# A decoder layer in float32 on one core: gate and up from seven half-size products instead of eight

## The chip, the cores and the metric

The kernel runs on one core of a Trainium2 chip. The metric is the device time in microseconds of one execution. A profiled execution leaves a trace, from which all rows below come.

## What is computed

One layer on 2048 tokens of 1024 values. Nearly all of its work is matrix products; the change touches the last line alone:

```python
h = rms_norm(x, attn_norm); proj = h @ w_in        # queries, keys, values, gates
y_dn = gated_deltanet_branch(...); y_swa = sliding_window_branch(...)
merged = gates[0] * (y_dn @ w_branch_dn) + gates[1] * (y_swa @ w_branch_swa)
x = x + merged @ w_out
h2 = rms_norm(x, ffn_norm)
x = x + (silu(h2 @ w_gate) * (h2 @ w_up)) @ w_down # D_FF = 2816
```

## The kernel before, in words

**Blocks.** The tokens are worked in four blocks of 512. Per block: the mixer (`mixer`: DeltaNet projections and cores, gates, branches), the output projection (`tok_gemm(("wo",))`), the norm before gate/up (`norm2`), then, for the *next* block, the key, value and query projections (`window_start`: `skv`, `sq`) and its sliding-window attention, and last gate/up and down in five parts of 4, 4, 4, 4 and 6 units. A unit f (`ffn_up`) is 128 rows of gate and of up, each the sum over eight slices of 128 inputs.

**Three products for one.** Every float32 operand is split into a high part `hi` in the rounded format float32r and the rest `lo = x - hi`; a product is hi·hi + hi·lo + lo·hi (`mm3`, L185). So a unit has 2 x 8 x 3 = 48 matmuls with 512 columns (tokens) moving over 128 x 128 weights.

**Weights.** `weights` (L154 to 183) gives the split weights. In block 0 it loads a raw tile `wraw` (2 buffers of 1 MB units), ACT copies out hi (L168), DVE or POOL in turn subtracts (L171), and the split tile `whl` is written to device memory (`wk`). Later blocks load `whl` as it is, 512 KB for half a unit of 1024 values. There are five `whl` buffers.

**Order.** TensorE's order is written by a planner: `drive` interleaves a dense generator (projections, gate/up, down) with side chains (attention, DeltaNet cores, norms), by an estimate of when each step is ready; the weight path goes by `self.raw` and is not in that estimate. The queues of ACT, DVE, POOL and of the DMAs (SP; some on ACT) are set by a scheduler. Every queue is in order. Tiles named `u` share `NU` slots; matmuls write eight banks (`acc`, `aux`).

**The end of a unit** (L889 to 904): ACT takes tanh of the gate's bank, DVE makes gate·(tanh + 1), multiplies by up's bank, ACT and DVE split the result into the pair `a` that down reads.

Most instructions carry line 109, which is the wrapper that records them; rows are told apart by their tiles: `h` the split activations, `a` the split result, `L`, `qT`, `kt`, `pT` attention's, `mt` the merged branches, `x` the residual.

Of the kernel before, what the change touches and what calls it, by code (L numbers as in the profile page):

```python
# [15 lines left out]
P = 128  # L16
# [12 lines left out]
NU = 63  # L29
ND = 6  # L30
WR = 2
WB = 5
PSUB = 2
# [81 lines left out]
class Emitter:  # L115
    def __init__(self, ctx, tc, ins, out, nblocks):
# [13 lines left out]
        self.kept = {}  # L130
        self.pacc = pool("acc", 8, space=bass.MemoryType.PSUM)
# [21 lines left out]

    def weights(self, key, a):  # L154
        nc = self.raw
        n = a * 264 if key[0] == "skv" else 1024
        h = a // 2
        hl = []
        if key not in self.kept:
            src = self.w_skv[key[1]] if key[0] == "skv" else self.w_all[UNITS[key]]  # L160
            raw = self.wp.tile([P, 1056], F32, name="wraw", tag="wraw", bufs=WR)
            nc.sync.dma_start(out=raw[:, :n], in_=src)
            keep = []
            for j in range(2):
                t = self.wp.tile([P, 2, 528], F32R, name="whl", tag="whl", bufs=WB)
                r = raw[:, j * n // 2:(j + 1) * n // 2]
                hi, lo = t[:, 0, :n // 2], t[:, 1, :n // 2]
                nc.scalar.activation(hi, r, AF.Copy)  # L168
                self.nsub += 1
                eng = nc.vector if self.nsub > 6 and self.nsub % PSUB else nc.gpsimd  # L170
                eng.tensor_tensor(out=lo, in0=r, in1=hi, op=ALU.subtract)  # L171
                if self.nblocks > 1:
                    d = self.kp.tile([P, 2, n // 2], F32, name="wk", tag="wk%d_%d" % (len(self.kept), j))
                    nc.sync.dma_start(out=d, in_=t[:, :, :n // 2].bitcast(F32))
                    keep.append(d)
                hl.append([t[:, e, :n // 2].rearrange("p (a m) -> p a m", a=h) for e in range(2)])
            self.kept[key] = keep
        else:
            for j in range(2):
                t = self.wp.tile([P, 2, 528], F32R, name="whl", tag="whl", bufs=WB)  # L180
                nc.sync.dma_start(out=t[:, :, :n // 2].bitcast(F32), in_=self.kept[key][j])
                hl.append([t[:, e, :n // 2].rearrange("p (a m) -> p a m", a=h) for e in range(2)])
        return lambda k: (hl[k // h][0][:, k % h], hl[k // h][1][:, k % h])
# [914 lines left out]
```

## Time and profile before

| | |
|---|---|
| median of 3 runs | 3195.55 us (3194.09 to 3197.91) |
| the profiled execution | 3196.13 us, its span 3194.3 us |
| busy: TensorE, VectorE, ScalarE, GpSimd | 3095.3, 1403.2, 837.6, 415.8 us |
| DMA | 596 MB, mean 187 GB/s |
| granted clock of TensorE | 0.99 on average |

The span runs from the first to the last instruction; the time is 1.8 us more. PE is TensorE's matmuls, PEld its weight loads, DVE VectorE, ACT ScalarE, POOL GpSimd. A matmul's busy time is its whole passage and overlaps the next one's; the distance from start to start is its pace. The 264-column projection (`skv`) of block 1 fills 1272 to 1280 us. In block 1 (the second block) the output projection begins at 1225 us, the attention of block 2 lies in 1325 to 1418, and the rest of gate/up and down goes to 1702; block 0 has the same stages from 441, 550 and 643 us on, and splits its weights there.

### The profile page before, as it was taken

The numbers are of one execution on the slowest core, as the hardware profiler recorded it, in microseconds if no ns is written. First come the engines' busy times: TensorE is split into PE (matmuls) and PEld (weight loads), VectorE is DVE, ScalarE is ACT, GpSimd is POOL, SyncE is SP. The second block draws the span as 40 slices with busy tenths as digits, with TensorE's granted clock in tenths as the row PEclk, the third lists the DMA queues.
The fourth block names the chain that finished last, engine by engine and source line by source line (L and its number), as shares of the span: only waits on it lengthen the run. The fifth ranks groups of instructions, "written<-read, shape, count | busy, mean of one in ns | idle before, by whom it ended". The sixth has DMA issues, their size and how long they took to land. (4 is left out here: it accounts for less than half of the span.)

```text
span 3194.3 us, 39761 instructions
## 1 busy us (share of the span) xinstructions
PE 3095.3 (97%) x14854; PEld 2523.6 (79%) x14854; DVE 1403.2 (44%) x3626; ACT 837.6 (26%) x2112; POOL 415.8 (13%) x401
## 2 busy tenths in 40 slices
PE   7888989999999999999999999999999999999999
PEld 5776778778888887878887888877888888878887
DVE  5867656533336544542215565443221655422221
ACT  4454334422323322330002323232000233110000
POOL 2433211322212100010001110011000211000000
PEclk9999999999999999999999999999999999999999
DMA  6554475588874446445556445545566544645565
GB/s 240 185 178 152 154 251 209 198 284 285 283 254 145 132 142 215 153 152 191 184 192 200 131 143 179 177 154 170 190 189 205 169 131 133 198 159 193 192 189 183
DMA packets 291848, 595.99 MB, mean 187 GB/s; under 512 B 18975, under 2 KB 20168, under 8 KB 291656
## 3 DMA queue, kind: packets, MB, share of 16 engines
q1 hardware_dynamic: 277648, 569.20, 54.1%
q10 hardware_dynamic: 14008, 24.25, 2.2%
q8 instruction: 117, 1.92, 0.2%
q14 instruction: 75, 0.61, 0.1%
HBM read 459.08 MB, written 134.30 MB: 186 GB/s over the span
## 5 line engine op out<-in xcount | busy, mean ns | idle before, releaser
L109 PE MATMUL acc<-h,whl 128*128 128x512 f32 x7296 | 1760.1, 397 | 7.5 <-DVE whl L171 4.9
L109 PEld LDWEIGHTS acc<-h,whl 128*128 128x128 f32 x7296 | 1357.6, 189 | 313.9 <-DVE whl L171 5.8
L109 PE MATMUL acc<-whl,a 128*128 128x512 f32 x2112 | 493.7, 393 | 0.0
L109 PEld LDWEIGHTS acc<-whl,a 128*128 128x128 f32 x2112 | 395.5, 188 | 90.3
L109 DVE TENSOR_TENSOR x<-x,acc 128x512 f32<-128x512 f32 x192 | 131.4, 687 | 390.4 <-PE acc L109 388.6
L171 POOL TENSOR_TENSOR whl<-wraw,whl 128x512 fp32r<-128x512 f32 (+1 forms) x123 | 167.0, 1359 | 565.4 <-ACT whl L168 472.6
L168 ACT ACTIVATE whl<-wraw 128x512 fp32r<-128x512 f32 (+1 forms) x240 | 149.0, 630 | 290.3 <-PE acc L109 136.1
L109 DVE TENSOR_TENSOR th<-th,acc 128x512 f32<-128x512 f32 x88 | 60.4, 687 | 316.0 <-PE acc L109 315.8
L109 DVE SCALAR_TENSOR_TENSOR th<-th,acc 128x512 f32<-128x512 f32 x88 | 60.5, 687 | 304.9 <-ACT th L109 304.9
L109 PE MATMUL acc<-whl,mt 128*128 128x512 f32 x768 | 181.9, 398 | 8.1 <-DVE h L109 7.6
L109 ACT ACTIVATE th<-acc 128x512 f32<-128x512 f32 x88 | 52.7, 598 | 499.5 <-PE acc L109 499.3
L109 PEld LDWEIGHTS acc<-whl,mt 128*128 128x128 f32 x768 | 145.9, 191 | 43.2 <-DVE h L109 8.5
L109 DVE SCALAR_TENSOR_TENSOR cv<-xr,cst_sb,cv 128x512 f32<-128x512 f32 x144 | 134.6, 935 | 60.7 <-ACT cv L109 53.1
L109 ACT ACTIVATE a<-th 128x512 fp32r<-128x512 f32 x88 | 55.5, 631 | 346.8 <-DVE th L109 332.1
L171 DVE TENSOR_TENSOR whl<-wraw,whl 128x512 fp32r<-128x512 f32 x117 | 89.8, 768 | 121.4 <-ACT whl L168 120.9
L109 PE MATMUL acc<-whl,h 128*128 128x264 f32 (+1 forms) x768 | 139.8, 341 | 0.0
L109 PEld LDWEIGHTS acc<-whl,h 128*128 128x128 f32 x768 | 118.0, 188 | 16.7 <-issue 1.1
L109 POOL COPY ccar<-xr 128x3 f32<-128x3 f32 x48 | 9.0, 188 | 858.5 <-ACT xr L109 858.5
L109 PE MATMUL acc<-sp,whl 128*128 128x512 f32 x384 | 103.2, 409 | 0.0
L109 POOL TENSOR_TENSOR pT<-pT,cst_sb 128x512 f32<-128x512 f32 x62 | 82.7, 1362 | 137.2 <-ACT pT L109 121.1
L109 ACT ACTIVATE L<-L,ast 128x256 f32<-128x256 f32 (+1 forms) x192 | 83.4, 457 | 60.0 <-DVE ast L109 60.0
L109 PE MATMUL acc<-ydn,whl 128*128 128x512 f32 x384 | 92.6, 401 | 0.4
(183 smaller groups left out, 2817.5 us busy)
## 6 DMA issues: line engine op xcount, KB each, us to landing
whl<-wk SPq DMA_DIRECT2D x708, 512.0 KB, 3.9
wk<-whl SPq DMA_DIRECT2D x236, 512.0 KB, 3.5
wraw<-in_w_all SPq DMA_DIRECT2D x118, 512.0 KB, 5.0
x<-in_x ACTq DMA_DIRECT2D x56, 256.0 KB, 5.1
out<-x ACTq DMA_DIRECT2D x32, 256.0 KB, 3.8
whl<-wk SPq DMA_DIRECT2D x12, 528.0 KB, 5.1
wk<-whl SPq DMA_DIRECT2D x4, 528.0 KB, 2.7
x<-in_x SPq DMA_DIRECT2D x8, 256.0 KB, 6.5
```

The lines of the kernel that those rows point to most:

```text
L109: r = f(*args, **kw)
L168: nc.scalar.activation(hi, r, AF.Copy)
L171: eng.tensor_tensor(out=lo, in0=r, in1=hi, op=ALU.subtract)
```

## The change

For blocks 1 to 3, gate and up of a unit are seen as a 2 x 2 matrix of quarters (A11, A12: gate, first and second half of the inputs; A21, A22: up) times a 2 x 2 matrix of the activations (B11, B12: first half of the inputs, tokens 0 to 255 and 256 to 511; B21, B22: second half). Seven products of quarters, with sums S1 to S4 of the weights and T1 to T4 of the activations, and seven additions on DVE and POOL of what they give replace the eight; each product is 4 x 3 matmuls of 256 columns (`ffn_seven`, `product`). The first two units of the last block (`PLAIN`) keep the eight products.

- Block 0 keeps the eight products, and also forms S1 to S4 of each unit (`four`: DVE two, POOL two) and writes these to device memory instead of split tiles.
- In later blocks a unit loads seven raw quarters of 256 KB (A11, A12, A22 from the input, S1 to S4 from device memory) and splits each (`seven`).
- `norm_S` forms and splits T1 to T4 after the norm (28 tiles of `u`); in the last block it also keeps the plain split for the two plain units.
- To make room, the activations `h` of the next block are written to device memory after `window_start` and read back when the last part's units are done (`refill`); both on ACT's DMA queue, 16 transfers of 256 KB each way, at three block ends.
- Raw tiles are half as large with eight buffers (`WR`), and stores of split tiles are issued after the next loads (`store_kept`).

The diff, cut to what the text below speaks of:

```diff
-NU = 63
+NU = 60
-WR = 2
+WR = 8
 WB = 5
+PLAIN = 2
...
+    def load_raw(self, src, n=TB):
+        raw = self.wp.tile([P, 528], F32, name="wraw", tag="wraw", bufs=WR)
+        self.raw.sync.dma_start(out=raw[:, :n], in_=src)
+        return raw[:, :n]
...
+    def split_raw(self, r, n=TB):
+        t = self.wp.tile([P, 2, 528], F32R, name="whl", tag="whl", bufs=WB)
+        hi, lo = t[:, 0, :n], t[:, 1, :n]
+        self.raw.scalar.activation(hi, r, AF.Copy)
+        self.either().tensor_tensor(out=lo, in0=r, in1=hi, op=ALU.subtract)
+        return t
...
+    def store_kept(self):
+        for d, t in self.unstored:
+            self.raw.sync.dma_start(out=d, in_=t)
+        self.unstored = []
...
+        if key in self.kept:
+            self.store_kept()
+            ts = [self.load_kept(d, n) for d in self.kept[key]]
+            raws = [self.load_raw(src[:, j * n:(j + 1) * n], n) for j in range(2)]
+            self.store_kept()
+            ts = [self.split_raw(r, n) for r in raws]
+            if self.nblocks > 1:
+                self.kept[key] = [self.keep(t[:, :, :n].bitcast(F32), [2, n]) for t in ts]
...
+    def four(self, keys):
+        v, gp = self.raw.vector, self.raw.gpsimd
+        got = {n: self.load_raw(self.quad(keys, m, h))
+               for n, m, h in (("A11", 0, 0), ("A12", 0, 1), ("A21", 1, 0), ("A22", 1, 1))}
+        self.store_kept()
+        def group(m):
+            hl = [[t[:, e, :TB].rearrange("p (a m) -> p a m", a=4) for e in range(2)]
+                  for t in [self.split_raw(got["A%d%d" % (m + 1, h + 1)]) for h in range(2)]]
+            return lambda k: (hl[k // 4][0][:, k % 4], hl[k // 4][1][:, k % 4])
+        def sums():
+            kept = self.kept[keys] = {}
+            for n, x, y, op, eng in (("S1", "A21", "A22", ALU.add, v), ("S2", "S1", "A11", ALU.subtract, v),
+                                     ("S3", "A11", "A21", ALU.subtract, gp), ("S4", "A12", "S2", ALU.subtract, gp)):
+                got[n] = self.u([TB], name="ws")
+                eng.tensor_tensor(out=got[n], in0=got[x], in1=got[y], op=op)
+                kept[n] = self.keep(got[n], [TB])
+        return group, sums
...
+    def seven(self, keys):
+        own = {"A11": (0, 0), "A12": (0, 1), "A22": (1, 1)}
+        self.store_kept()
+        def of(name):
+            t = self.split_raw(self.load_raw(self.quad(keys, *own[name]) if name in own else self.kept[keys][name]))
+            return [t[:, e, :TB].rearrange("p (a m) -> p a m", a=4) for e in range(2)]
+        return of
...
+    def product(self, ps, w, H, operand, start=True):
+        mm = self.nc.tensor.matmul
+        for k in range(4):
+            hi, lo = H[k][operand]
+            for i, (l, r) in enumerate(((w[0], hi), (w[0], lo), (w[1], hi))):
+                mm(ps, l[:, k], r, start=start and k == 0 and i == 0, stop=k == 3 and i == 2, skip_group_check=not start)
+            yield 0
...
+            f1, f2 = fs.pop(k), fs.pop(k + 4)
+            (b11, b12), (b21, b22) = [(f[:, 0], f[:, 1]) for f in (f1, f2)]
+            ta, tb = [self.u([2, 256], name="hs") for _ in range(2)]
+            gp.tensor_tensor(out=ta[:, 0], in0=b12, in1=b11, op=ALU.subtract)
+            gp.tensor_tensor(out=ta[:, 1], in0=b22, in1=ta[:, 0], op=ALU.subtract)
+            v.tensor_tensor(out=tb[:, 0], in0=b22, in1=b12, op=ALU.subtract)
+            v.tensor_tensor(out=tb[:, 1], in0=b21, in1=ta[:, 1], op=ALU.subtract)
+            if hs is None:
+                one = self.u([2, 256], F32R, name="hb")
+                nc.scalar.activation(one[:, 0], b11, AF.Copy)
+                v.tensor_tensor(out=one[:, 1], in0=b11, in1=one[:, 0], op=ALU.subtract)
+                o = {"B11": (one[:, 0], one[:, 1])}
+                two = split(f2, v)
+            else:
+                o = {"B11": tuple(e[:, 0:256] for e in hl[k])}
+                two = [e.rearrange("p (a n) -> p a n", a=2) for e in hl[k + 4]]
+            for names, (hi, lo) in ((("B21", "B22"), two), (("T1", "T2"), split(ta, v)), (("T3", "T4"), split(tb, gp))):
+                for i, n in enumerate(names):
+                    o[n] = (hi[:, i], lo[:, i])
...
+        if b == 0:
+            yield from self.norm_T(xns, self.g2, hs)
+        else:
+            yield from self.norm_S(xns, self.g2, H, hs if b + 1 == self.nblocks else None)
...
+        keys = (("up", f, 0), ("up", f, 1))
+        if b == 0:
+            group, sums = self.four(keys)
+        elif b + 1 == self.nblocks and f < PLAIN:
+            group, sums = lambda m: self.raw_weights(keys[m]), lambda: None
+        else:
+            return self.ffn_seven(H, keys)
+        return self.ffn_eight(hs, group, sums)
...
+        yield lambda: len(H) == 4
+        w = self.seven(keys)
+        half = (slice(0, 256), slice(256, 512))
+        bank = lambda: self.acc()[:, 0:256]
+        Y = bank()
+        yield from self.product(Y, w("S2"), H, "T2")
+        c = self.u([2, 256], name="pc")
+        nc.scalar.activation(c[:, 1], Y, AF.Copy)
+        G = bank()
+        yield from self.product(G, w("A11"), H, "B11")
+        nc.scalar.activation(c[:, 0], G, AF.Copy)
+        U = self.u([2, 256], name="pu")
+        gp.tensor_tensor(out=U[:, 0], in0=c[:, 0], in1=c[:, 1], op=ALU.add)
+        Z = bank()
+        yield from self.product(Z, w("S1"), H, "T1")
+        yield from self.product(Y, w("S3"), H, "T3", start=False)
+        v.tensor_tensor(out=U[:, 1], in0=c[:, 0], in1=Y, op=ALU.add)
+        th = self.u([TB], name="th")
+        up = self.u([TB], name="up")
+        v.tensor_tensor(out=up[:, half[1]], in0=U[:, 1], in1=Z, op=ALU.add)
+        yield from self.product(G, w("A12"), H, "B21", start=False)
+        nc.scalar.activation(th[:, half[0]], G, AF.Tanh, scale=0.5)
+        v.scalar_tensor_tensor(out=th[:, half[0]], in0=th[:, half[0]], scalar=1.0, in1=G, op0=ALU.add, op1=ALU.mult)
+        yield from self.product(Y, w("A22"), H, "T4", start=False)
+        v.tensor_tensor(out=up[:, half[0]], in0=c[:, 0], in1=Y, op=ALU.add)
+        yield from self.product(Z, w("S4"), H, "B22", start=False)
+        v.tensor_tensor(out=U[:, 0], in0=U[:, 0], in1=Z, op=ALU.add)
+        nc.scalar.activation(th[:, half[1]], U[:, 0], AF.Tanh, scale=0.5)
+        v.scalar_tensor_tensor(out=th[:, half[1]], in0=th[:, half[1]], scalar=1.0, in1=U[:, 0], op0=ALU.add, op1=ALU.mult)
+        v.tensor_tensor(out=th, in0=th, in1=up, op=ALU.mult)
+        return self.ffn_act(th)
...
+        if b:
+            self.put = []
+            for k, h in enumerate(hs):
+                self.put.append([])
+                for e in range(2):
+                    d = self.kp.tile([P, TB], F32, name="hk", tag="hk%d_%d" % (k, e))
+                    nc = self.raw
+                    nc.scalar.dma_start(out=d, in_=h[e].bitcast(F32))
+                    self.put[-1].append(d)
+            hs.clear()
+    def refill(self, hs):
+        for d in self.put:
+            h = self.pair("h")
+            for e in range(2):
+                self.raw.scalar.dma_start(out=h[e].bitcast(F32), in_=d[e])
+            hs.append(h)
+            yield 1500
...
-        yield lambda: kv.scales
+        yield lambda: kv.scales and len(hs) == KT
...
+                if last and more:
+                    h2.clear()
+                    h4.clear()
+                    self.spawn(self.refill(hs))
```

**How it moves instructions.** First TensorE in block 1, after attention, one part of four units and down's parts around it (`hb`: the split sums of the activations). Before:

```order
L109 MATMUL acc<-h,whl 128x512 x27
L109 MATMUL aux<-pT,vt 64x512 x4
L109 MATMUL acc<-h,whl 128x512 x123
L109 MATMUL acc<-whl,a 128x512 x96
L109 MATMUL acc<-h,whl 128x512 x192
L109 MATMUL acc<-whl,a 128x512 x96
```

After:

```order
L110 MATMUL acc<-hb,whl 128x256 x69
L110 MATMUL acc<-whl,a 128x512 x9
L110 MATMUL aux<-pT,vt 64x512 x4
L110 MATMUL acc<-whl,a 128x512 x87
L110 MATMUL acc<-hb,whl 128x256 x336
L110 MATMUL acc<-whl,a 128x512 x96
L110 MATMUL acc<-hb,whl 128x256 x336
```

Four units are 336 matmuls of 256 columns instead of 192 of 512; down's are the same.

Second ACT in the same part of block 1 (whole queue; `th` tanh, `a` the split result, `pc` the copies of the banks Y and G, `pu` and `acc` what tanh reads). Before:

```order
L109 ACTIVATE a_13257<-th_13224 128x512 [waits DVE_49]
L109 ACTIVATE th_13290<-acc_13265 128x512 [waits PE_49]
L109 ACTIVATE a_13323<-th_13290 128x512 [waits DVE_49,Activation_49]
L109 ACTIVATE th_13356<-acc_13331 128x512 [waits PE_49,Activation_49]
L109 ACTIVATE a_13389<-th_13356 128x512 [waits DVE_49,Activation_49]
```

After, a little more than one unit (the tile of A22, the result of the unit before, the two copies, S4, then the next unit's quarters):

```order
L110 ACTIVATE th_15678<-pu_15640 128x256 [waits DVE_49]
L169 ACTIVATE whl_15844<-wraw_15842 128x512 [waits DMAHW3_49,PE_49,Pool_49]
L110 ACTIVATE a_15739<-th_15678 128x512 [waits DVE_49]
L110 ACTIVATE pc_15761<-acc_15743 128x256
L110 ACTIVATE pc_15761<-acc_15763 128x256 [waits PE_49]
L169 ACTIVATE whl_15862<-wraw_15860 128x512 [waits DMAHW4_49,Activation_49]
L169 ACTIVATE whl_15888<-wraw_15886 128x512 [waits DMAHW5_49,PE_49,Pool_49]
L169 ACTIVATE whl_15908<-wraw_15906 128x512 [waits DMAHW6_49,PE_49,Activation_49]
L110 ACTIVATE th_15820<-acc_15763 128x256 [waits PE_49]
L169 ACTIVATE whl_15929<-wraw_15927 128x512 [waits DMAHW7_49,Pool_49]
L169 ACTIVATE whl_15946<-wraw_15944 128x512 [waits DMAHW0_49,DVE_49,PE_49]
L169 ACTIVATE whl_15967<-wraw_15965 128x512 [waits DMAHW1_49,PE_49,Pool_49]
```

Seven splits a unit and four steps of 256 columns stand where two instructions stood; the split of S4 comes behind the copies here, and ahead of them in every other unit.

Third ACT at the end of block 0's gate/up and in its last down part, where weights are split for the first time. Before:

```order
L109 ACTIVATE a<-th 128x512
L168 ACTIVATE whl<-wraw 128x512
L109 ACTIVATE th<-acc 128x512
L168 ACTIVATE whl<-wraw 128x512 x3
L109 ACTIVATE a<-th 128x512
L168 ACTIVATE whl<-wraw 128x512 x4
```

After:

```order
L110 ACTIVATE a<-th 128x512
L169 ACTIVATE whl<-wraw 128x512
L110 ACTIVATE th<-acc 128x512
L169 ACTIVATE whl<-wraw 128x512 x3
L110 ACTIVATE a<-th 128x512
L1120 DMA h<-hk 128x512 x16
L169 ACTIVATE whl<-wraw 128x512 x4
L1205 DMA out<-x 128x512 x2
```

All 16 transfers that bring `h` back stand ahead of seven of the twelve splits of this down part.

## Rows read from the trace of the kernel before

**Rows 1.** Page, part 1: busy time, share and instructions of each engine.

```profile
PE 3095.3 (97%) x14854; PEld 2523.6 (79%) x14854; DVE 1403.2 (44%) x3626; ACT 837.6 (26%) x2112; POOL 415.8 (13%) x401
```

**Rows 2.** Waits of TensorE, whole span: us in total, times, longest.

```profile
PE acc L109 <- DVE whl L171: 4.9, 2, 3.1
PE acc L109 <- POOL whl L171: 1.3, 1, 1.3
```

**Rows 3.** Timeline of TensorE, block 1, gate/up: start us, us, engine, what, count.

```profile
1468.81 44.65 PE L109 MATMUL acc<-h,whl 128*128 128x512 f32 x192
1513.30 22.33 PE L109 MATMUL acc<-whl,a 128*128 128x512 f32 x96
```

**Rows 4.** Windows: us; busy of PE, PEld, DVE, ACT, POOL; clock; DMA share; GB/s.

```profile
1272.00:1280.00 8.00, 8.00 (x68) 8.00 (x67) 5.40 (x21) 0.45 (x2) 0.00 (x0) 1.00 0.79 249
```

**Rows 5.** Timeline of TensorE, block 0, attention's score matmuls and the next group.

```profile
621.42 2.23 PE L109 MATMUL aux<-kt,qT 128*128 128x256 f32 x16
623.49 0.40 PE L109 MATMUL acc<-h,whl 128*128 128x512 f32 x1
```

**Rows 6.** Weight loads in 1272 to 1280 us: count | busy, mean ns | idle.

```profile
L109 PEld LDWEIGHTS acc<-whl,h 128*128 128x128 f32 x67 | 8.2, 188 | 0.0
```

**Rows 7.** Groups by line and shape: count | busy, mean ns | idle before.

```profile
L168 ACT ACTIVATE whl<-wraw 128x512 fp32r<-128x512 f32 x236 | 146.7, 630 | 290.0 <-PE acc L109 136.1 <-DMA wraw<-in_w_all 84.4 <-issue 48.7
L171 DVE TENSOR_TENSOR whl<-wraw,whl 128x512 fp32r<-128x512 f32 x117 | 89.8, 768 | 121.4 <-ACT whl L168 120.9
L171 POOL TENSOR_TENSOR whl<-wraw,whl 128x512 fp32r<-128x512 f32 x119 | 162.0, 1362 | 552.7 <-ACT whl L168 460.0 <-DVE G L109 26.3 <-PE aux L109 21.2
L109 ACT ACTIVATE T<-aux 64x256 f32<-64x256 f32 x16 | 6.0, 374 | 6.7 <-PE aux L109 6.2
L109 DVE TENSOR_TENSOR L<-L 128x256 f32<-128x256 f32 x60 | 25.2, 421 | 29.9 <-ACT L L109 29.1
L109 DVE TENSOR_TENSOR th<-th,acc 128x512 f32<-128x512 f32 x88 | 60.4, 687 | 316.0 <-PE acc L109 315.8
L109 ACT ACTIVATE L<-L,ast 128x256 f32<-128x256 f32 x120 | 59.4, 497 | 47.5 <-DVE ast L109 47.5
L109 DVE SCALAR_TENSOR_TENSOR h<-aux,cst_sb,h 128x512 fp32r<-128x512 f32 x64 | 43.7, 744 | 3.7 <-ACT h L109 3.2
```

**Rows 8.** Windows by stage; columns as in rows 4.

```profile
441.00:487.00 46.00, 43.55 (x189) 34.97 (x188) 15.70 (x24) 14.46 (x29) 7.97 (x6) 1.00 0.82 285
550.00:643.00 93.00, 87.49 (x405) 66.00 (x404) 52.64 (x167) 47.74 (x138) 37.78 (x31) 0.98 0.53 183
643.00:894.00 251.00, 251.00 (x1085) 203.67 (x1085) 81.04 (x120) 75.67 (x125) 58.70 (x46) 1.00 0.83 285
1224.00:1271.00 47.00, 46.10 (x194) 37.40 (x195) 10.18 (x15) 8.17 (x21) 0.00 (x0) 0.96 0.61 201
1325.00:1418.00 93.00, 92.15 (x458) 71.69 (x456) 46.72 (x170) 37.66 (x118) 22.03 (x21) 1.00 0.45 144
1418.00:1669.00 251.00, 251.00 (x1087) 203.81 (x1086) 50.93 (x76) 20.72 (x35) 0.00 (x0) 1.00 0.59 188
```

**Rows 9.** Timeline of TensorE, block 3: transposes, then the first gate/up.

```profile
2817.66 6.15 PE L109 MATMUL aux<-cst_sb,xn 128*128 128x128 f32 x32 [4.64 <-DVE xn L109]
2823.57 44.69 PE L109 MATMUL acc<-h,whl 128*128 128x512 f32 x192
```

**Rows 10.** ACT's DMA issues of x, 1200 to 1260 us: count: duration ns min/median/max.

```profile
L356 ACTq DMA_DIRECT2D x<-in_x x10: 334/361/680, 1200.5 to 1226.1; - x10
```

**Rows 11.** Timeline, block 1, the end of a unit of gate/up: DVE, then ACT, then DVE.

```profile
1491.28 0.69 DVE L109 TENSOR_TENSOR th<-th,acc 128x512 f32<-128x512 f32 x1 [4.23 <-PE acc L109]
1492.00 0.64 ACT L109 ACTIVATE a<-th 128x512 fp32r<-128x512 f32 x1 [5.67 <-DVE th L109]
1492.67 0.69 DVE L109 SCALAR_TENSOR_TENSOR a<-th,a 128x512 fp32r<-128x512 f32 x1 [0.70 <-ACT a L109]
```

More of the change, by code (lines that the diff above doesn't have):

```diff
@@ new lines, in keep, with load_kept @@
+    def keep(self, t, shape):
+        d = self.kp.tile([P] + shape, F32, name="wk", tag="wk%d" % self.nkept)
+        self.nkept += 1
+        self.unstored.append((d, t))
+        return d
+    def store_kept(self):
+        for d, t in self.unstored:
+            self.raw.sync.dma_start(out=d, in_=t)
+        self.unstored = []
+    def load_kept(self, d, n=TB):
+        t = self.wp.tile([P, 2, 528], F32R, name="whl", tag="whl", bufs=WB)
+        self.raw.sync.dma_start(out=t[:, :, :n].bitcast(F32), in_=d)
+        return t
@@ L154, in weights @@
     def weights(self, key, a):
-        nc = self.raw
-        n = a * 264 if key[0] == "skv" else 1024
+        n = (a * 264 if key[0] == "skv" else 1024) // 2
         h = a // 2
+        src = self.w_skv[key[1]] if key[0] == "skv" else self.w_all[UNITS[key]]
         hl = []
[L159 to L177, printed above, removed]
-        else:
[L179 to L182, printed above, removed]
@@ new lines, in weights, with quad @@
+        for t in ts:
+            hl.append([t[:, e, :n].rearrange("p (a m) -> p a m", a=h) for e in range(2)])
+        return lambda k: (hl[k // h][0][:, k % h], hl[k // h][1][:, k % h])
+    def quad(self, keys, m, h):
+        return self.w_all[UNITS[keys[m]]][:, h * TB:(h + 1) * TB]
+    def four(self, keys):
[15 more added lines that the diff above has]
+        return group, sums
@@ L351, in norm_T, with norm_S, turned, split @@
             yield 0
+    def norm_S(self, xns, gain, H, hs):
+        nc, v, gp = self.nc, self.nc.vector, self.nc.gpsimd
+        fs, hl = {}, {}
+        def turned(kk):
+            ps = self.aux()
+            for t in range(NT):
+                nc.tensor.transpose(ps[:, t * P:(t + 1) * P], xns[t][kk // 4][:, (kk % 4) * P:(kk % 4 + 1) * P], self.ident)
+            f = fs[kk] = self.u([2, 256], name="hf")
+            ff, g = f.rearrange("p a n -> p (a n)"), gain[:, kk:kk + 1]
+            if hs is None:
+                nc.scalar.activation(ff, ps, AF.Copy, scale=g)
+                return
+            hl[kk] = h = self.pair("h")
+            nc.scalar.activation(h[0], ps, AF.Copy, scale=g)
+            v.scalar_tensor_tensor(out=h[1], in0=ps, scalar=g, in1=h[0], op0=ALU.mult, op1=ALU.subtract)
+            if kk % 2:
+                nc.scalar.activation(ff, ps, AF.Copy, scale=g)
+            else:
+                v.tensor_scalar(out=ff, in0=ps, scalar1=g, scalar2=None, op0=ALU.mult)
+        def split(src, eng):
+            hi, lo = [self.u([2, 256], F32R, name="hb") for _ in range(2)]
+            nc.scalar.activation(hi, src, AF.Copy)
+            eng.tensor_tensor(out=lo, in0=src, in1=hi, op=ALU.subtract)
+            return hi, lo
+        if hs is not None:
+            for kk in range(KT):
+                turned(kk)
+                hs.append(hl[kk])
+                yield 0
+        for k in range(4):
+            for kk in (k, k + 4) if hs is None else ():
+                turned(kk)
+                yield 0
+            f1, f2 = fs.pop(k), fs.pop(k + 4)
[5 more added lines that the diff above has]
+            v.tensor_tensor(out=tb[:, 1], in0=b21, in1=ta[:, 1], op=ALU.subtract)
+            if hs is None:
+                one = self.u([2, 256], F32R, name="hb")
[9 more added lines that the diff above has]
+                    o[n] = (hi[:, i], lo[:, i])
+            H.append(o)
+            yield 0
@@ L378, in norm2 @@
         yield
-        yield from self.norm_T(xns, self.g2, hs)
+        if b == 0:
+            yield from self.norm_T(xns, self.g2, hs)
+        else:
+            yield from self.norm_S(xns, self.g2, H, hs if b + 1 == self.nblocks else None)
         yield
@@ L896, in ffn_up @@
         v.scalar_tensor_tensor(out=th, in0=th, scalar=1.0, in1=pg, op0=ALU.add, op1=ALU.mult)
-        w = self.weights(("up", f, 1), 8)
+        w = group(1)
+        sums()
         pu = self.acc()
```

32 lines of the change are left out of this document (23 added, 9 removed).

## The prediction

> **What bounds the kernel now.** I read the busy totals first: TensorE is busy for 97% of the span, and the next engine, VectorE, for 44% [rows 1]. Then the waits of TensorE: the long ones lie at the start, in the first block, and before the last block's gate/up; in the first block 4.9 and 1.3 us are waits for a weight tile that is still being split [rows 2]. So the time is the number of TensorE's instructions times their pace, and the pace is read from a stretch without gaps. In the second block's gate/up, 192 matmuls of 512 columns start at 1468.81 and the next stage starts at 1513.30: 44.49 / 192 = 0.2317 us each [rows 3]. One unit f (128 rows of gate and of up) has 48 of them, 11.12 us. A matmul's busy time is no pace, as the ends overlap the next start. Last I read the stages, for what lies idle beside TensorE [rows 8].
>
> **TensorE's gain.** 64 units (22, 22 and 20 in blocks 1, 2, 3, counted from 0) go from 48 matmuls of 512 columns to 84 of 256. The columns fall by an eighth; what matters is the price of 256. Three rows bound it. The 264-column projection ran 66 starts in 8.00 us (two of the 68 counted had begun before): 0.1212 [rows 4]; carried eight columns down along the line from 512 to 264 columns it is 0.1176. The attention's 16 score matmuls of 256 columns took 2.07 us from their first start to the next group, 0.1294 with their three changes of bank [rows 5]. I take 0.120, nearest the 264-column row, because a product is also a gapless run of twelve into one bank. A unit then costs 84 x 0.120 = 10.08 us and saves 1.04 us; 64 units save **66.6 us** (79 at 0.1176, 16 at 0.1294).
>
> In that 264-column stretch weight loads last 188 ns each [rows 6] while a new matmul starts every 121 ns and TensorE shows no gap: loads lie under earlier matmuls. [...]
>
> **The splits of the weights.** A unit in blocks 1 to 3 now loads seven raw quarters and splits each: ACT 7 x 0.630 = 4.4 us, and 3.5 subtractions each on DVE (0.768, 2.7 us) and POOL (1.362, 4.8 us) [rows 7]. Two copies and two tanh of 256 columns at 0.374 and the activation's 0.63 bring ACT to 6.5 us of 10.1; six DVE steps of 256 columns (0.421), a multiply and a difference (0.69 each) bring DVE to 6.6. No engine is full. A product lasts 1.44 us; five buffers leave four products, 5.8 us, between a freed buffer and its next use, against 0.63 + 1.36. Loads fall from 2.1 to 1.8 MB a unit. In the gapless stage I cost the splits at nothing; the cover is those 5.8 us.
>
> The tight place is ACT's turn. Product 4 adds into bank Y, so it waits for the copy of Y, which stands behind the last unit's activation and, in every other unit, behind the split of S4, which waits for product 2. Product 2 ends 2.9 us into the unit; 0.17 until its result is out (0.285 less 0.120), split 0.63, copy 0.37: 4.1 us, against product 4's start at 4.3. The other branch (DVE 0.42, tanh 0.37, DVE 0.42 and 0.69, ACT 0.63, hops of 0.03 to 0.1 [rows 11]) ends at 3.0 and fits too. I put **+2 us** for places where it doesn't; bounds 0 and the second rival.
>
> **Attention beside gate/up** (blocks 1 and 2). There ACT and DVE work for the attention's chain too, whose steps TensorE takes in a fixed order. Block 0 shows what splits do to it: in 550 to 643 us, with four splits a unit, TensorE was busy 87.49 of 93 us; in the same stage of block 1, without splits, 92.15 [rows 8]. So four splits cost 4.65 us, and seven in a shorter unit at 1.9 times the rate some 9. But the new order also leaves more matmuls between the chain's steps (75 short ones, 9.0 us, where 30 of 0.23, 7.0 us, stood). I take 7 a block, **+14 us** (bounds 0 and 59, the third rival).
>
> **Forming the activation's sums.** In block 3, eight transposed groups now get a third copy: DVE 0.744 plus half of a pass over a bank (0.687), against 0.77 a group before (6.15 / 8) [rows 7, 9]: +2.6 us. The sums lie under the two plain units (22 us). In blocks 1 and 2 they lie beside the 81 query matmuls (18.8 us); four rounds of about 3.8 us on ACT fit, and waiting banks cost 1 us each. **+4.6 us** (2 to 12).
>
> **The activations of the next block go out and come back.** 16 transfers of 262 KB each way, 4.2 MB, at three block ends, all issued by ACT at 0.36 us each [rows 10]. On the way out they lie in the output projection. In block 0 that stage moved 285 GB/s at a share of 0.82, so about 347 is full; 91 more is 376, and 17.3 MB take 50 us instead of 46: +4. In blocks 1 and 2, 201 + 89 fits [rows 8], but the activations behind these issues on ACT come later: +1 each. On the way back, block 0 has all 16 standing in ACT's queue before the split of the sixth of twelve down tiles. Issue alone holds ACT for 5.8 us, and waiting for half of them to land another 6; they start about 3 us into the part (the last unit's end chain above), and the sixth tile's split must begin at 9.8 us (two pairs of tiles at 24 x 0.2317, three matmuls, less 0.63 and 1.36): 0 to 5 late, I take 3. In the other blocks nothing of the part stands behind them, and 188 + 127 GB/s fits. **+9 us** (0 to 30).
>
> **Block 0.** Raw loads in halves with eight buffers, and stores behind the next loads, should remove most of the 6.2 us of waits for weights: **-4** (-6.2 to +3). The four sums a unit (DVE 2 x 0.69, POOL 2 x 1.36) lie under 11.1 us on engines that are 32% and 23% busy there [rows 8], and attention's part costs **+1** (0 to 8).
>
> **Sum.** -66.6 + 2 + 14 + 4.6 + 9 - 4 + 1 = -40.0. The profiled execution took 3196.1 us (span 3194.3 and 1.8 around it), 0.6 above the median of the runs: **3156 us**.
>
> **Rivals.**
> 1. Weight loads set the pace. At 188 ns a piece a unit costs 84 x 0.188 = 15.8 us, 4.7 more than before: 3196 + 300 + 27 = 3523 us. For it: TensorE's load row is busy for 8.00 of 8.00 us in the 264-column stretch. Against it: the same stretch has no gap at 121 ns. Chance 0.02. [...]
> 2. **Slower: ACT's turn sets the period.** If a subtraction of 0.77 on DVE stands before the add that ends product 7 and another before the multiply, the copy of Y comes 1.5 us later, 1.2 past product 4's start, in every unit: 77 us, 3233 us. It decides from 0.6 us past the margin on, as 40 us / 64 is what a unit has to lose. For it: in-order queues and a margin of 0.2 us. Against it: in the order of DVE these subtractions stand where ACT has already waited, and the hops are short. Chance 0.12.
> 3. No change: each of the eight attention tiles waits for a whole run of eight exponentials (4.0 us) and eight additions (3.4): 59 us instead of 14, 3201 us. For it: block 0's 5.5 idle us. Against it: the wider gaps. Chance 0.14.
> 4. The transfers are not hidden: 4.2 MB at 347 GB/s is 12 us, six times 72 instead of 9: 3219 us. Against it: the mean rate of a block doesn't rise. Chance 0.05.
>
> **How the numbers follow.** My forecast's own course has 0.67 and lies between 3125 (0.1176, half of the losses) and 3182 (0.1244 a matmul). With the third rival's 3201 the range is **3125 to 3205**; outside stay the other rivals and part of the low end. About 6 us (0.2%) is what a measurement tells from no change: faster is below 3189, slower above 3202. Faster: 0.67, half of rival 3 and a part of 4: 0.77. Slower: rivals 1 and 2, and parts of 3 and 4: 0.17. The same: 0.06.
>
> **What would show it.** In the second block's gapless gate/up: 336 matmuls of 256 columns in 40.3 us, four units, where 192 took 44.5. At 42 us or more the price or rival 2 is at work; then TensorE's waits name ACT or DVE behind `pc`, or a late weight tile. The stage from the query projection to the end of attention tells rival 3 by its idle time, block 0's last down part the refill, by a wait for a tile that ACT splits late. Fewer than 1 us saved a unit, or more than 20 us of new waits in attention, makes me wrong. [...]

## The result, and the profile after

The changed kernel took **3212.82 us** (median of 4 runs, 3209.78 to 3218.35) against 3195.79 in the same comparison: a ratio of 1.0059, 95% interval 1.0047 to 1.0071. It is slower by 17 us where I forecast 40 less. The profiled execution has a span of 3210.7 us, 16.4 more than before. Its busy totals, as [rows 1]:

```profile
PE 3054.8 (95%) x17158; PEld 2594.7 (81%) x17158; DVE 1831.4 (57%) x4258; ACT 1174.2 (37%) x2804; POOL 876.8 (27%) x773
```

TensorE is busy for 40 us less and the time is longer all the same: the gain was made, and idle time was put in. The table shows where: lengths of stages in us, from the starts of TensorE's matmuls in each trace (blocks 1 and 2 as a pair). The "attention stretch" runs from a block's first gate/up matmul to the first of the third down part: 12 units, two down parts, and in blocks 0 to 2 the next block's attention (the expectations below, which name its end loosely, mean this stretch). The "dense stretch" goes on to the last down part: 10 units, two down parts.

| stage | before | changed | a5: splits on DVE | a3: six split tiles | k2: best |
|---|---|---|---|---|---|
| block 0, up to gate/up | 515.4 | 514.4 | 490.8 | 512.2 | 485.1 |
| block 0, attention stretch | 210.5 | 216.6 | 210.3 | 213.6 | 220.5 |
| block 0, last down part | 33.0 | 41.4 | 42.0 | 41.2 | 33.6 |
| 1, 2: wo's end to gate/up | 40.5, 40.5 | 43.2, 43.2 | 41.7, 43.3 | 43.3, 41.7 | 43.3, 41.7 |
| 1, 2: attention stretch | 202.2, 202.3 | 213.6, 212.9 | 199.7, 199.4 | 205.5, 205.6 | 199.5, 198.2 |
| 1, 2: dense stretch | 155.4, 155.4 | 144.6, 145.9 | 144.4, 145.2 | 144.6, 146.1 | 143.0, 143.1 |
| 1, 2: last down part | 33.0, 33.0 | 36.2, 37.3 | 38.5, 39.3 | 33.1, 33.1 | 33.1, 33.1 |
| block 3, first stretch | 177.7 | 173.3 | 172.8 | 173.9 | 170.7 |
| block 3, dense stretch | 155.4 | 145.9 | 144.9 | 146.5 | 143.4 |
| block 3, last down part | 33.0 | 33.1 | 33.4 | 33.1 | 33.1 |

The dense stretches give what was forecast. In TensorE's timeline of block 1, four units (336 matmuls) go from 1501.24 to 1541.20, 0.1189 us a start, where [rows 3] had 44.49 us; two rows above stand the 5.15 us that were lost beside attention:

```profile
1334.32 0.96 PE L110 MATMUL acc<-hb,whl 128*128 128x256 f32 x6
1340.43 10.80 PE L110 MATMUL acc<-hb,whl 128*128 128x256 f32 x75 [5.15 <-DVE pu L110]
...
1501.24 40.12 PE L110 MATMUL acc<-hb,whl 128*128 128x256 f32 x336
1541.20 4.08 PE L110 MATMUL acc<-whl,a 128*128 128x512 f32 x17
```

The windows of block 1, columns as in [rows 4], say the same: 17.7 us without TensorE in the attention stretch (214 less 196.27), where the kernel before had 0.85, and almost none in the dense one. First the changed kernel, then the one before:

```profile
1327.00:1350.00 23.00, 17.85 (x134) 17.51 (x133) 17.54 (x33) 10.69 (x23) 7.64 (x7) 0.85 0.35 105
1327.00:1541.00 214.00, 196.27 (x1367) 176.32 (x1366) 140.74 (x320) 103.94 (x255) 89.75 (x74) 0.97 0.45 144
1541.00:1686.00 145.00, 144.65 (x1037) 135.34 (x1036) 83.45 (x131) 61.08 (x120) 54.60 (x45) 1.00 0.59 185
```

```profile
1311.00:1513.00 202.00, 201.15 (x929) 160.09 (x928) 74.02 (x220) 48.70 (x138) 22.03 (x21) 1.00 0.53 168
```

The granted clock is the second loss: 0.97 over 214 us, up to 6 us. After the 5.15 us wait, 75 matmuls took 10.80 us, 0.144 each, at a granted clock of 0.83.

TensorE's waits over the whole span (us in total, times, longest) name what is new, beside attention's own:

```profile
PE acc L110 <- DMA whl<-wk: 17.9, 18, 2.2
PE acc L110 <- DVE pu L110: 12.6, 7, 5.2
...
PE acc L110 <- ACT whl L169: 8.4, 4, 6.1
...
PE acc L110 <- ACT pc L110: 4.0, 5, 1.6
PE acc L110 <- POOL whl L170: 3.5, 6, 0.9
```

Late split tiles (the last row) are little. The 5.15 us are read on DVE and POOL at that place; product 6 waits for `pu`, the add that reads bank Y:

```profile
1332.77 1.29 POOL L170 TENSOR_TENSOR whl<-wraw,whl 128x512 fp32r<-128x512 f32 x1 [0.22 <-ACT whl L169]
1332.85 1.27 DVE L110 TENSOR_TENSOR qst<-qst 128x32 f32<-128x32 f32 x1
...
1335.98 1.36 DVE L110 SCALAR_TENSOR_TENSOR qst<-qst 128x32 f32<-128x32 f32 x2
1336.02 1.28 POOL L170 TENSOR_TENSOR whl<-wraw,whl 128x512 fp32r<-128x512 f32 x1 [1.96 <-ACT whl L169]
1337.38 2.50 DVE L110 TENSOR_TENSOR qr<-qr,qst 128x512 f32<-128x512 f32 x4
...
1339.96 0.41 DVE L110 TENSOR_TENSOR pu<-pc,acc 128x256 f32<-128x256 f32 x1
```

The chain `qst`, `qr` (the query norm of attention) stands ahead of `pu` in DVE's queue. Its steps of 32 elements take 0.19 us where nothing is beside them, and 1.27 here: they end when POOL's subtraction ends (1332.77 + 1.29 = 1334.06; 1332.85 + 1.27 = 1334.12). Here that adds 2.0 us ahead of `pu` (1.27 for 0.19, 1.36 for 0.42). The four `qr` steps, 2.50 us at their usual length, stand there by the order of the queue alone; so the hold and the order share this wait. The groups of the changed kernel show it in sum (count | busy, mean ns | idle before):

```profile
L170 DVE TENSOR_TENSOR whl<-wraw,whl 128x512 fp32r<-128x512 f32 x345 | 303.4, 880 | 207.4 <-ACT whl L169 189.1 <-DMA wraw<-in_w_all 15.7
L110 DVE SCALAR_TENSOR_TENSOR th<-th,pu 128x256 f32<-128x256 f32 x64 | 54.7, 855 | 19.8 <-ACT th L110 19.8
L110 DVE TENSOR_TENSOR pu<-pc,acc 128x256 f32<-128x256 f32 x64 | 26.7, 417 | 38.1 <-PE acc L110 38.1
```

Two steps of 256 columns, one at 417 ns and one at 855. So I had two theories of the attention stretch to test, that splitting more weights costs as such, or that the seven products' own chain is held up on DVE, and three causes for the rest: POOL's hold on DVE, too few split tiles, the transfers in ACT's queue.

### The profile page after: what moved, and what is told of

Same layout as the page of the kernel before. It is cut to its first block, busy times and chain, and to the rows that moved or that the text cites. A ratio compares the mean times of both kernels' runs of the same rounds, so it can differ in the third digit from the quotient of the medians.

```text
span 3210.7 us, 47669 instructions
## 1 busy us (share of the span) xinstructions
PE 3054.8 (95%) x17158; PEld 2594.7 (81%) x17158; DVE 1831.4 (57%) x4258; ACT 1174.2 (37%) x2804; POOL 876.8 (27%) x773
## 5 line engine op out<-in xcount | busy, mean ns | idle before, releaser
L110 PE MATMUL acc<-h,whl 128*128 128x512 f32 (+1 forms) x4944 | 1140.2, 383 | 5.4 <-DVE whl L170 1.8
L110 PEld LDWEIGHTS acc<-h,whl 128*128 128x128 f32 x4944 | 872.3, 190 | 179.5 <-issue 3.3
L170 POOL TENSOR_TENSOR whl<-wraw,whl 128x512 fp32r<-128x512 f32 (+1 forms) x351 | 473.9, 1352 | 1128.0 <-ACT whl L169 975.9
L169 ACT ACTIVATE whl<-wraw 128x512 fp32r<-128x512 f32 (+1 forms) x696 | 432.9, 629 | 609.1 <-PE acc L110 438.5
L110 PE MATMUL acc<-hb,whl 128*128 128x256 f32 x4656 | 577.3, 282 | 22.7 <-DVE pu L110 12.6
L110 PEld LDWEIGHTS acc<-hb,whl 128*128 128x128 f32 x4656 | 561.4, 190 | 32.4 <-DVE pu L110 17.9
L110 PE MATMUL acc<-whl,a 128*128 128x512 f32 x2112 | 503.8, 397 | 23.2 <-DMA whl<-wk 16.9
L170 DVE TENSOR_TENSOR whl<-wraw,whl 128x512 fp32r<-128x512 f32 x345 | 303.4, 880 | 207.4 <-ACT whl L169 189.1
L110 POOL TENSOR_TENSOR hs<-hf 128x256 f32<-128x256 f32 x12 | 12.6, 1050 | 320.6 <-ACT hf L110 320.6
L110 DVE SCALAR_TENSOR_TENSOR th<-th,acc 128x256 f32<-128x256 f32 (+1 forms) x88 | 43.3, 492 | 78.7 <-ACT th L110 78.5
```

What stands on the lines that cost most here:

```text
L110: r = f(*args, **kw)
L169: self.raw.scalar.activation(hi, r, AF.Copy)
L170: self.either().tensor_tensor(out=lo, in0=r, in1=hi, op=ALU.subtract)
```

## The experiments

Each is timed against the kernel before in the same job; ratios are with their 95% interval.

**a2: the transfers spread out.**

```diff
-                    self.spawn(self.refill(hs))
+                    bring = self.refill(hs)
...
+                for _ in range(2):
+                    next(bring, 0)
```

(the second piece stands in `tok_gemm`, after each weight tile)

> The changed kernel, but the 16 transfers that bring h back are issued in pairs between the weight tiles of the last down part, not all at its start. Theory (they hold ACT's queue for 16.3 us, so the splits of block 0's last down part come late and TensorE stands 6.1 us and then runs at a lower granted clock): block 0's last down part falls from 41.4 us to 34 to 36, the whole to about 3206 us. Rival (the transfers cost by their bytes, wherever they are issued): that part stays above 40 us and the time at 3212.

3210.09 us, 1.0057 (1.0042 to 1.0072). Block 0's last down part took 38.9 us, between the two forecasts; block 2's took 40.6 instead of 37.3, and the whole time is not told apart from the changed kernel's. In that part of the changed kernel's block 0 TensorE stood 6.10 us, and the granted clock from 911 to 921 us was 0.66. ACT's timeline of the changed kernel, and of this run:

```profile
900.10 0.63 ACT L110 ACTIVATE a<-th 128x512 fp32r<-128x512 f32 x1
900.16 16.33 ACTq L1120 DMA_DIRECT2D h<-hk  x16
916.54 2.19 ACT L169 ACTIVATE whl<-wraw 128x512 fp32r<-128x512 f32 x4 [15.81 <-DMA h<-hk]
```

```profile
899.18 9.29 ACTq L1122 DMA_DIRECT2D h<-hk  x8
908.57 0.63 ACT L169 ACTIVATE whl<-wraw 128x512 fp32r<-128x512 f32 x1 [8.82 <-DMA wraw<-in_w_all]
909.45 4.28 ACTq L1122 DMA_DIRECT2D h<-hk  x4
```

The scheduler still put eight ahead, and these hold ACT for 9.3 us. The transfers back hold the queue; that they cost nothing elsewhere isn't shown by this.

**a3: six split tiles.**

```diff
-WR = 8
-WB = 5
+WR = 6
+WB = 6
```

> The changed kernel with six split tiles and six raw half tiles instead of five and eight. Theory (a down part's first tile finds its buffer free only four short products before it is wanted, and its 512 KB take 5 to 6.5 us to land): TensorE's waits for tiles loaded from device memory fall from 17.9 us to under 5, the time by 10 to 3203 us. Rival (the loads are slow because the transfers are full then): those waits stay above 12 us and the time within 4 us of 3212.

3181.78 us, 0.9971 (0.9961 to 0.9981): faster than before, three times the effect forecast. The waits for tiles from device memory:

```profile
PE acc L110 <- DMA whl<-wk: 3.6, 6, 1.2
```

The last down parts of blocks 1 and 2 are back at 33.1 us, with the same transfers of `h` beside them. Block 3's has five split tiles in the changed kernel, but no such transfers, and takes 33.1 us as well: the 3.2 and 4.3 us need both, the transfers and the five tiles. The attention stretches lose 8.1 and 7.2 us.

**a4: eight products, split anew.**

```diff
-            yield from self.norm_S(xns, self.g2, H, hs if b + 1 == self.nblocks else None)
+            yield from self.norm_T(xns, self.g2, hs)
...
-        elif b + 1 == self.nblocks and f < PLAIN:
+        else:
             group, sums = lambda m: self.raw_weights(keys[m]), lambda: None
-        else:
-            return self.ffn_seven(H, keys)
```

> Blocks 1 to 3 compute gate and up by the eight full products again, from the plain split of the activations, but load four raw quarters a unit and split them anew; the sums of the weights are still formed and stored in block 0, but not read. No sums of the activations. Theory A (what slows the stage beside attention is the splitting of weights as such): the stretch from the first gate/up matmul to the end of the second down part, 202.2 us before and 213.6 with seven, takes 210 or more in blocks 1 and 2, and the time is 3195 + 13 (block 0) + 16 + some = 3225 or more. Theory B (it is the seven products' own chain: banks that wait for adds behind attention's work on DVE): the stretch takes 203 to 206 us, and the time is 3208 to 3216.

3217.54 us, 1.0080 (1.0065 to 1.0095). The stretch is 204.25 and 204.21 us, theory B, though the time lies 1.5 us above B's range; block 1's window:

```profile
1328.00:1532.00 204.00, 201.93 (x929) 160.23 (x928) 93.30 (x242) 74.65 (x183) 53.70 (x44) 1.00 0.35 108
```

Four splits a unit beside attention cost 2 us a block, with POOL subtracting as in the changed kernel. The loss needs the seven products' chain or the other three splits of a unit; this run has neither, so it doesn't separate the two. For the chain speak the changed kernel's waits in block 1's stretch: 6.1 us for `pu`, none of which the kernel before had, and 2.1 for split tiles.

**a5: subtractions on DVE.**

```diff
-        return self.raw.vector if self.nsub > 6 and self.nsub % PSUB else self.raw.gpsimd
+        return self.raw.vector
```

> The changed kernel with all subtractions of the weight splits on DVE, none on POOL. Theory (a DVE instruction that meets one of POOL's 1.3 us subtractions lasts until that one ends, as the trace shows with 194 of DVE's own subtractions at 1.03 us instead of 0.69 and the tanh products at 1.29 instead of 0.42): DVE's means fall back to 0.69 and 0.42, its busy total stays under 2000 us, the stretch of blocks 1 and 2 falls from 213.6 to 200 to 206 us, the time to 3185 to 3200. Rival (DVE's queue is what is full beside attention, and 351 more instructions of 0.69 us make it longer): the stretch grows to 218 or more and the time to 3225 or more.

3159.84 us, 0.9897 (0.9882 to 0.9912). The theory holds and forecast too little: the stretches, 199.7 and 199.4 us, lie just below its range, the time 25 us below. DVE's groups and block 1's windows are

```profile
L170 DVE TENSOR_TENSOR whl<-wraw,whl 128x512 fp32r<-128x512 f32 x692 | 497.8, 725 | 245.9 <-ACT whl L169 236.4 <-DMA wraw<-in_w_all 0.7
L110 DVE TENSOR_TENSOR pu<-pc,acc 128x256 f32<-128x256 f32 x64 | 26.9, 420 | 23.2 <-PE acc L110 21.2
L110 DVE SCALAR_TENSOR_TENSOR th<-th,pu 128x256 f32<-128x256 f32 x64 | 26.9, 420 | 7.5 <-ACT th L110 7.2
```

```profile
1296.00:1496.00 200.00, 190.09 (x1367) 171.31 (x1365) 146.06 (x362) 103.12 (x254) 35.12 (x33) 1.00 0.50 156
```

The scheduler's queues changed with this edit, too. At the place of the 5.15 us wait, `pu` now stands ahead of `qr`:

```profile
1302.54 0.41 DVE L110 TENSOR_TENSOR pu<-pc,acc 128x256 f32<-128x256 f32 x1
...
1304.29 2.49 DVE L110 TENSOR_TENSOR qr<-qr,qst 128x512 f32<-128x512 f32 x4
```

So the run alone doesn't show that it is POOL, nor how the gain divides between POOL's hold and the order; d1, where `pu` stands ahead of `qr` as well, tests the hold. DVE makes 347 more subtractions, and is busy for 92 us more in all (1923.8 against 1831.4), not for the 240 that they take at 0.69. The clock is back at 1.00. But 24 us of the gain lie in block 0 ahead of gate/up, where nothing of the change is but the half raw tiles and the order of the loads and stores. Hence the next run.

**c1: the kernel before, subtractions on DVE.** The same edit in the kernel before (L170).

> The kernel before, with all subtractions of the weight splits on DVE. Theory (POOL's subtractions hold up DVE wherever weights are split, also in the kernel before; the 24 us that the first block's mixer gave in the changed kernel have nothing to do with the seven products): the mixer of block 0 falls from 428 to about 404 us, blocks 1 to 3 stay within 1 us, the time falls to 3163 to 3172. Rival (the gain needs the half raw tiles and the later stores of the changed kernel): the time stays above 3185.

3174.88 us, 0.9943 (0.9929 to 0.9958); block 0's mixer 409.0 us instead of 427.9, the stages of blocks 1 to 3 within 0.6. The theory holds, 3 us short of its range: POOL's subtractions cost the kernel before 19 us, too. Against this fairer base a5 is 15 us faster, not 33.

**d1: POOL's subtraction for nothing.**

```diff
-        self.either().tensor_tensor(out=lo, in0=r, in1=hi, op=ALU.subtract)
+        self.raw.vector.tensor_tensor(out=lo, in0=r, in1=hi, op=ALU.subtract)
+        self.nsub += 1
+        if self.nsub > 6 and self.nsub % PSUB == 0:
+            self.raw.gpsimd.tensor_tensor(out=self.idle[:, :n], in0=r, in1=hi, op=ALU.subtract)
```

> All split subtractions on DVE, and beside every second of them POOL makes the same subtraction once more into a scratch tile that nobody reads (seven raw half tiles instead of eight, to make room for it). Theory (POOL's instruction holds up DVE's while it runs): though every tile of weights is finished by DVE, the gain of the run with DVE's splits goes again: the first block's mixer back from 402 to 415 or more, the stretch of blocks 1 and 2 from 199.5 to 207 or more, the time to 3190 or more. Rival (that gain came from the tiles, which POOL finished 0.67 us later than DVE does): the time stays at 3155 to 3170.

3333.32 us, 1.0440 (1.0423 to 1.0458). The rival is out: every tile is finished by DVE and nobody reads POOL's copy, yet block 0's mixer takes 435 us, the attention stretches of blocks 1 and 2 grow to 229 and the dense ones to 162 us. It is far more than forecast. Here the two subtractions of a tile become ready together, and 316 of POOL's 345 copies overlap a subtraction of DVE:

```profile
L171 DVE TENSOR_TENSOR whl<-wraw,whl 128x512 fp32r<-128x512 f32 x692 | 692.7, 1010 | 236.6 <-ACT whl L170 233.2 <-DMA wk<-whl 0.2
```

The size is not the hold's alone, as a copy also keeps its raw tile from being loaded anew: the queue of the loads waits 108 times, 134.6 us in all, for a copy to end, and ACT waits 116.5 us for raw tiles, where it waited 6.8 in a5. How the 173 us between d1 and a5 divide between the two isn't shown.

**k2: the cures together.**

```diff
-NU = 60
-WR = 8
-WB = 5
+NU = 62
+WR = 4
+WB = 6
...
+        return self.raw.vector
...
-        if b:
+        if b > 1:
             self.put = []
...
-                    self.spawn(self.refill(hs))
+                    if b:
+                        self.spawn(self.refill(hs))
```

> The changed kernel with all split subtractions on DVE, six split tiles and four raw half tiles, 62 slots of u, and h of the second block kept on the chip through block 0 (no transfers at block 0's end; at the two later ends as before). Theory (the causes are separate and add up): block 0's last down part 33 us, the stretch from the first gate/up to the second down part 190 to 196 in blocks 1 and 2, the last down parts there 33 to 34, the time 3118 to 3132. Rival (with four raw tiles the raw loads come late, and waits for splits take the place of the others): the stretch stays at 199 or more and the time above 3140.

**3126.16 us**, 0.9790 (0.9776 to 0.9805): 2.1% faster than before, and 49 us below c1, which has DVE's splits without the seven products. Block 0's last down part is 33.6 us, the others 33.1. The attention stretches (199.5, 198.2) miss the 190 to 196, one of them on the rival's side, and block 0's grew to 220.5; the time lies in its range all the same, which is in part luck. The fewer raw tiles or other slots may be what costs there; d2, d3 and k6 vary them.

**k4: transfers back in POOL's queue** (a5 and a3 together, and in `refill`:)

```diff
-                self.raw.scalar.dma_start(out=h[e].bitcast(F32), in_=d[e])
+                self.raw.gpsimd.dma_start(out=h[e].bitcast(F32), in_=d[e])
```

> As the one before, but with six raw half tiles and 60 slots, h goes out in block 0 too, and the transfers that bring it back stand in POOL's queue, which has nothing else then. Theory (only the holding of ACT's queue cost time): block 0's last down part 33 to 34 us, the time 3118 to 3132, equal to the one before within 5 us. Rival (the 4.2 MB themselves get in the way of the raw loads of that part, as 9.3 us for the first eight issues in the run with spread transfers suggest): that part stays at 38 us or more.

3132.10 us, 0.9811 (0.9796 to 0.9825). Block 0's last down part takes 35.9 us, between the two forecasts: some 5.4 of its 8.4 were ACT's queue, 2.9 stay, for the transfers by this reading. In blocks 1 and 2 that part is now 37.6 and 37.7 us, with waits for tiles from device memory (three in block 1, 3.8 us) despite six split tiles; a3 and k2, which issue the transfers from ACT's queue, have 33.1 there, so from POOL's queue they do get in the way. The attention stretches are 195.3 and 196.6, the size that the prediction's own sum gave for them (202.2 less 12.5, 7 more for attention: 196.7). With all subtractions on DVE and the sixth tile nothing is left above the forecast; k2, which has both and fewer raw tiles, keeps 1.5 to 2.8 us. What makes up the 7 is not what was forecast: in block 1 TensorE waits 4.1 us for `pc` and `pu` and 2.6 for attention's tiles.

**k5: the products' steps ranked first** (k2, and around each step of `ffn_seven` on ACT, DVE and POOL:)

```diff
+        with self.tc.high_priority(700):
```

> As k2, with the steps of the seven products on ACT, DVE and POOL (copies of the banks, adds, tanh, products) put ahead of attention's in the scheduler's ranking. Theory (TensorE's waits for pu and pc beside attention come from in-order queues in which attention's chain was ranked first): these waits fall from some 5 us a block to under 2, and the time is 4 to 10 us below k2. Rival (the scheduler does not see these steps as ready earlier, or attention's own tiles then come later by as much): within 3 us of k2.

3136.31 us, 0.9823 (0.9806 to 0.9839), 10 above k2: the theory is out, and the loss is more than the rival's. The waits for `pc` and `pu` did not fall (9.6 and 2.1 us in all, 9.9 and 2.1 in k2), and TensorE's waits for attention's `L` on DVE grew from 1.2 to 9.2 us. Why the waits for `pc` stay is open.

**d2, d3, k6: how to share the memory.** All on k2: d2 five raw tiles, 61 slots, all four sums of block 0 on DVE; d3 the same with six raw, five split tiles, 62 slots; k6 is d2 with the sums as they were.

```diff
-                                     ("S3", "A11", "A21", ALU.subtract, gp), ("S4", "A12", "S2", ALU.subtract, gp)):
+                                     ("S3", "A11", "A21", ALU.subtract, v), ("S4", "A12", "S2", ALU.subtract, v)):
```

> As k2, with five raw half tiles and 61 slots of u, and the four sums of the weights in block 0 all on DVE. Theory (k2's first stretch of block 0, 220.5 us against 210.3 with eight raw tiles, is long because the four raw tiles of a unit are held until its sums are made, two of them by POOL at 1.36 us each): that stretch falls to 208 to 214 and the time to 3112 to 3122. Rival (it is DVE, which takes the sums as well): it stays at 218 or more and the time at 3126.

> As the one before, with six raw half tiles, five split tiles and 62 slots. Theory (the sixth split tile is what takes away the waits for down's first tiles, in the attention stretch and in the last down parts): the last down parts of blocks 1 and 2 go back from 33.06 to 36 or more, the stretches there from about 198 to 200 or more, while block 0's stretch is at most 211. The time is 3120 to 3132. Rival (raw tiles count as much as split tiles): within 3 us of the one before.

> As k2, with five raw half tiles and 61 slots of u; the four sums of the weights in block 0 two on DVE and two on POOL again. Theory A (the run with all four sums on DVE was slow in block 0's first stretch, 228.6 us, because of DVE's four more steps ahead of attention's): the stretch falls to 212 to 217 and the time to 3117 to 3124, below k2. Theory B (few raw tiles and few slots are what makes that stretch long): it stays at 220 or more and the time at 3126 or more.

3136.91 us, 0.9821 (0.9807 to 0.9836); 3142.46, 0.9840 (0.9826 to 0.9855); 3131.84, 0.9810 (0.9793 to 0.9828). None beats k2; k6's interval overlaps k2's. Block 0's stretch is 228.6, 215.0 and 227.0 us: neither the raw tiles alone nor DVE's sums explain 220.5, d2's theory falls, and k6's numbers are theory B's. 61 slots gave 227 and more, 62 gave 215 to 222 (k5), but 60 with `h` sent out and DVE's splits 210 and 215 (a5, k4); what decides there stays open. d3's time and block 0's stretch miss its forecast, and block 2's stretch is 199.9, but it confirms the sixth split tile: without it the last down parts are 38.6 and 38.3 us again.

## Why the prediction was wrong, step by step

By the stages of the two profiled executions the change is +16.6 us: -63.8 for 64 units (at the 0.997 us a unit of the dense stretches, 29.9 us for 30 units), +46.0 in the attention stretches, +17.2 for the transfers' stages, +11.9 around the activation's sums, +4.7 in block 0, +0.6 in the mixers.

- **What bounds the kernel, TensorE's gain: right.** 0.1189 us a matmul was forecast as 0.120. The first rival is out: in the changed kernel from 1501.24 to 1541.20 us loads of 188 ns in all 128 rows stand beside a new matmul every 119 ns, with no gap. How the loads come to lie under the matmuls isn't shown.
- **Attention beside gate/up: wrong, 46 us for 14 (and 2 for ACT's turn).** The step that failed is the cost of this stage: I charged it with attention's own waits, scaled from block 0's idle time by the number of splits, and put the waits of the seven products' chain there (beyond the +2 for the whole kernel), and any loss of clock, at nothing. In block 1 attention's own waits grew from 0.8 to 3.1 us; the others are 6.1 for `pu`, 4.7 for down's tiles, 2.1 for split tiles and 1.4 for `pc`, and the granted clock was 0.97, where [rows 8] have 1.00. a4 shows that four splits a unit cost 2 us a block, not 4.65.
- **The price of a DVE step: wrong, and behind the waits for `pu`.** I took 0.768 us for a subtraction from [rows 7] and 0.421 for the 256-column steps as if they were properties of those steps. 0.768 was the mean of 80 that ran alone (0.69) and 37 that met one of POOL's instructions (0.94), and the 60 steps behind 0.421 met none. With POOL subtracting 3.5 times a unit, 197 of DVE's 345 subtractions met one (1.02 us), and so did half of the `th<-th,pu` steps (1.29) and some of `qst`; the steps that read a bank kept their 0.42, but stand behind these in the queue. In the seven products' chain such a step frees a bank that is wanted 1.4 us later; in eight products nothing is that near. DVE's splits, with the order that came with them, took back 13.9 and 13.5 us of 23.4 and 22.6.
- **The splits' cover: wrong by what it left out.** "Five buffers leave four products, 5.8 us" was set against a split alone. The down tiles use the same buffers, and the 512 KB of one took 6.5 us to land in that stretch. The sixth tile (in a3, with six raw tiles for eight) took back 8.1 and 7.2 us there, and beside the transfers the 3.2 and 4.3 us of the last down parts.
- **The transfers: 17.2 for 9, and in other places.** On the way out I had 6 us, and the output projections grew by 1.3. On the way back ACT was held for 16.3 us, not 5.8 + 6, and block 0's part grew by 8.4, not 3. The other two parts grew by 3.2 and 4.3 where I had nothing: the transfers run beside down's tiles, and with five buffers these came late.
- **The sums of the activation: 11.9 for 4.6.** They are not hidden: 2.7 and 2.6 us ahead of gate/up in blocks 1 and 2, and in block 3 a longer gap, six short waits for `h` (2.3 us) and, at the first unit of seven, the copy's turn on ACT:

```profile
2848.28 6.19 PE L110 MATMUL aux<-cst_sb,xn 128*128 128x128 f32 x32 [5.69 <-DVE xn L110]
...
2857.73 0.50 PE L110 MATMUL acc<-h,whl 128*128 128x512 f32 x1 [0.47 <-ACT h L110]
...
2886.42 1.68 PE L110 MATMUL acc<-hb,whl 128*128 128x256 f32 x12 [1.58 <-ACT pc L110]
```

- **Block 0: +4.7 for -3.** The half tiles gained 1.4 us in the mixer; the attention stretch lost 6.0, which a5 takes back with POOL's subtractions alone (its sums stay).
- **The rivals.** The third (3201 us) named the right stage and the wrong mechanism: attention's own waits grew by 2.3 us a block, not by 30. The second put a hold-up of 1.5 us on DVE into every unit, and its mechanism, a late add, is the one that happened, but beside attention only; the dense units kept their 10 us. I let DVE's margins rest on means.

## What to carry to other kernels

A mean duration is a price only for the neighbours it was measured beside (0.768 us here stood for 0.69 alone and 0.94 beside POOL): look at an operation's least and longest before you put hundreds more of them on a neighbouring engine. When a change shortens the distance between steps that free a bank, each engine's busy share says little (DVE's was 57% here); the in-order queue ahead of the freeing step says more. And count every user of a shared set of buffers, not only the one that the change adds.

## What the runs showed of the hardware

- Some operations of DVE and POOL lasted longer when they met. In the changed kernel `th<-th,pu`, whose operands are both `u` tiles, takes 410 ns at least, 602 in the median, 1494 at most: the 32 that met one of POOL's instructions took 1.29 us in the mean, the other 32 took 0.42. With no split on POOL (a5) it takes 411, 418, 426. `pu<-pc,acc`, which reads a matmul's bank, takes 405, 421, 423 and 407, 422, 423, though 58 of the 64 in the changed kernel met POOL. In d1 POOL is slower as well: 1629 ns a subtraction, where it took 1352 in the changed kernel. Two of four `TENSOR_SCALAR` steps of `qst` on float32, with one tile as input, took 1.17 us instead of 0.18 beside POOL, too. What sets apart the operations that do this isn't shown.
- In block 0 of the changed kernel a stretch at a lower granted clock cost more than the short wait ahead of it. A wait of 1.25 us is followed, about a microsecond later, by pairs of 128-column matmuls 0.43 us apart instead of 0.22, until 552.4: eight pairs, some 1.6 us more. The granted clock from 549.0 to 552.4 is 0.50 of full speed. What lowers it isn't shown.

```profile
546.10 0.39 PE L110 MATMUL aux<-kcar,qT 128*128 128x128 f32 x2
546.32 0.39 PE L110 MATMUL aux<-kt,qT 128*128 128x128 f32 x2
547.95 0.44 PE L110 MATMUL aux<-kcar,qT 128*128 128x128 f32 x2 [1.25 <-DVE qT L110]
...
549.38 0.63 PE L110 MATMUL aux<-kt,qT 128*128 128x128 f32 x2
549.80 0.63 PE L110 MATMUL aux<-kcar,qT 128*128 128x128 f32 x2
```

- Sixteen transfers of 256 KB issued in a row held ACT's queue for 16.3 us in the changed kernel, eight of them 9.3 us in a2, where an issue alone takes 0.36 [rows 10]; POOL's queue took 4.4 us for its first eight in k4.
